# Hybrid attention encoder: low parts of turned probabilities and of meta keys on GpSimd, inverse sums half a tile sooner

## The chip, the core and the metric

The kernel runs on one core of a Trainium2 chip. Times are device microseconds (us) of one execution. The core has a matmul engine (TensorE, PE in the profile), a vector engine (VectorE, DVE), a scalar engine (ScalarE, ACT), a general engine (GpSimd, POOL) and SyncE (SP), which issues the DMA transfers here. Each engine works through its own queue in order; an instruction that waits holds back all that stand behind it.

## The reference

Two layers of a transformer-like block on 512 tokens of a grid 64 wide, with 16 meta tokens ahead of them, D = 1024, all in float32:

```python
def hybrid_layer(x, norm_g, w_in, q_norm_g, k_norm_g, rpb, w_o_attn, w_o_na, w_out, cos, sin):
    h = rms_norm(x, norm_g)
    proj = jnp.einsum('bld,de->ble', h, w_in)
    qa, ka, va, za, qb, kb, vb, zb, ga, gb = split_cols(proj)
    qa = apply_axial_rope(rms_norm(qa.reshape(b, l, ATTN_HEADS, HEAD_DIM), q_norm_g), cos, sin)
    ka = apply_axial_rope(rms_norm(ka.reshape(b, l, ATTN_KV_HEADS, HEAD_DIM), k_norm_g), cos, sin)
    ...
    oa = gqa_attention(qa, ka, va) * jax.nn.silu(za)
    ...
    ob = neighbourhood_attention(qb, kb, vb, rpb) * jax.nn.silu(zb)
    ya = jnp.einsum('ble,ed->bld', oa, w_o_attn)
    yb = jnp.einsum('ble,ed->bld', ob, w_o_na)
    mixed = jax.nn.sigmoid(ga) * ya + jax.nn.sigmoid(gb) * yb
    return x + jnp.einsum('bld,de->ble', mixed, w_out)
```

`gqa_attention` is the global branch: 8 query heads, 2 key heads, softmax over all 528 keys. `neighbourhood_attention` is the window branch: 8 heads, each query sees a window of 8 x 16 grid neighbours and the meta keys.

## The kernel before

**Precision.** Every matmul operand is split into a high part, a float32r cast, and a low part, the difference. A product is three matmuls: high by high, high by low, low by high (lines 325 to 327 in `product`).

**The main stream.** Each layer streams 58 chunks of weights through TensorE. A chunk comes in two halves of 128x512: the raw weights by DMA (line 235), the high part `whi` by a cast on ScalarE (line 240), the low part `wlo` by a subtraction on GpSimd (line 241). `weights` keeps three halves ahead of the product that needs them. The product of a chunk covers the tokens in two spans of 264 where the meta tokens are still needed (layer 0, and the keys and values of layer 1) and else in one span of 512; a span of the first kind, and half of one of the second, is half a tile of work and ends with a `tick`.

**The side work.** The attention branches run beside this stream. Two objects of the class `Side` hold the units of the global branch (`side_gqa`) and the heads of the window branch (`side_na`). At each tick they write down the steps that are due; a unit starts every four ticks, and its steps stand at numbers of ticks after its start, in the tables `GQA_AT` and `NA_AT`. A scheduler then orders each engine's queue from the written order, priorities and what waits for what.

**A unit of the global branch** (`global_unit`) is one query head and a pair of 128-query blocks; there are 16 in each layer, and two smaller ones of the meta queries in layer 0. Its steps:

- *scores*: two matmul groups into `S` (lines 556, 557), scaling and maximum on VectorE (837), exponential on ScalarE (841) into `P`, with the sums of the exponentials in `suma`.
- *turn*: P is transposed in blocks of 32 on VectorE (867) and written to DRAM (870). *back*: four reads bring it back turned (877), one more the rows of the meta keys (880, tile `pm`).
- *split*: each of two `split_part` casts half of the turned P to `pth` on ScalarE (193) and subtracts to `ptl` on VectorE (194), both in the helper `split`. *ends*: `split_ends` does the same for the meta keys' rows, two casts of 32x128 on ScalarE (896) and two subtractions on VectorE (898), into a kept tile `ga`.
- *sums*: nine matmuls (905) of values by `pth`, `ptl` and `ga` into `av`. ScalarE and VectorE then collect it into the branch's output (`combine`, lines 769 and 773).

**Inverse sums.** The probabilities aren't divided; instead the gate `za` of a pair of heads is multiplied by the inverse sums. The last unit of a pair carries the three steps of `divided_later`: *turned* takes the reciprocal (808), transposes it (809) and writes it with four DMAs (811); *spread* reads it back to all partitions with two (817); *multiplied* multiplies `za` on GpSimd (822). `gated` (777) then multiplies the output by za. The table's entry "divide" places these three. The window branch has its own entry and its own copy of the steps, with `zb`.

**A head of the window branch** (`windowed_head`) writes scores over a bias tile, transposes the probabilities on TensorE in three steps (tiles `ta`, `tb`, `tc`, line 129), splits them (`tah`/`tal`, `tbh`/`tbl`, line 194), and in layer 0 also moves a small tile of meta probabilities, `tm` to `mm` (lines 1019, 1020). The transposed tiles share a few PSUM banks, so that a transposition waits until an earlier tile has been read. Its values are split into `VB`.

GpSimd has the 210 `wlo`, and beside them the multiplications of line 822, the split of the windows' keys (533, tile `KB`) and of their queries (514), and the last products' kept weights (272).

Of the kernel before, what the change touches and what calls it, by code (L numbers as in the profile page):

```python
# [11 lines left out]
F32 = mybir.dt.float32  # L12
# [21 lines left out]
DEPTH = 2  # L34


GQA_AT = ({"scores": (0, 1), "turn": (1, 2), "back": 3, "split": (5, 5), "ends": 5, "divide": (3, 4, 6), "sums": (7, 7)},
          {"scores": (0, 1), "turn": (1, 2), "back": 3, "split": (5, 5), "ends": 5, "divide": (3, 4, 6), "sums": (7, 7)})
NA_AT = ({"stages": (0, 2, 5, 5, 5, 7), "values": (3, 4), "divide": (3, 4, 6)},
         {"stages": (0, 2, 4, 5, 5, 7), "values": (3, 4), "divide": (3, 4, 6)})  # L40

# [54 lines left out]
def trunk_kernel(ctx: ExitStack, tc: tile.TileContext, xT, w, gn, gf, bias, rope, out):  # L96
    nc = tc.nc
# [15 lines left out]
    def slot(tag, name, dt=F32):  # L113
        n = NKEY if tag in ("KB", "KR", "K", "E") else NTOK
        t = slots.tile([P, n], dt, tag=tag, bufs=BUFS[tag], name=name)
        return t[:, :NTOK] if tag == "E" else t
# [54 lines left out]
    def pad_tile(kind):  # L171
        padded[kind].rotate(1)
        return padded[kind][0]
# [14 lines left out]

    split_at = {}

    def split(hi, lo, src):
        with tc.high_priority():
            split_at["hi"] = nc.scalar.copy(hi, src)  # L193
            split_at["any"] = nc.vector.tensor_sub(lo, src, hi.bitcast(F32))  # L194

    def newton(out, x, tmp):
        nc.vector.scalar_tensor_tensor(tmp, out, -0.5, out, op0=ALU.mult, op1=ALU.mult)
# [236 lines left out]
    first, ends = {}, ((0, HALF), (HALF, NTOK))  # L434
# [19 lines left out]
    for l in range(DEPTH):  # L454
# [22 lines left out]
        def rotated(c, g, full, name):  # L477

            n, j = NTOK if full else NREAL, c - QA

            if name == "k":
                keys.append(slot("KR", f"{name}{l}_{c}")[:, :NTOK + NMETA])
            q = slot("E", f"{name}{l}_{c}") if name == "q" else keys[0][:, NMETA:]
            sq = slot("G", f"{name}s{l}_{c}")
            qh, ql = slot("G", f"{name}h{l}_{c}", F32R), slot("G", f"{name}l{l}_{c}", F32R)
            for ps, a, b in project(c, full):
                with ExitStack() as held:
                    if "last" in evac:
                        held.enter_context(tc.issue_after(evac["last"].ins))
                    nc.scalar.mul(q[:, a:b], ps, g)  # L490
                    nc.scalar.activation(qh[:, a:b], ps, AF.Square)
                    evac["last"] = nc.scalar.activation(sq[:, a:b], ps, AF.Square)
            with tc.high_priority():
                evac["low"] = nc.vector.tensor_sub(ql[:, :n], sq[:, :n], qh[:, :n].bitcast(F32))
            side_gqa.later(NORM_AT[l]["squares"][j], lambda: sum_squares(j, n, qh, ql))

            def rotate():
                sh = slot("G", f"{name}r{l}_{c}")
                nc.vector.stream_shuffle(sh[:, :n], q[:, :n], [(i + 16) % 32 for i in range(32)])
                nc.vector.tensor_mul(sh[:, :n], sh[:, :n], sin[:, :n])  # L500
                nc.vector.tensor_mul(q[:, :n], q[:, :n], cos[:, :n])
                nc.vector.tensor_add(q[:, :n], q[:, :n], sh[:, :n])

            return q, rotate
# [86 lines left out]
        qs, turn = [], None  # L591
        for j in range(4):
# [3 lines left out]
            with tc.issue_after(evac["low"].ins):  # L596
                if l == 0 and j == 0:
                    turn = rotate
                else:
                    if turn:  # L600
                        turn()
                    turn = None
# [14 lines left out]
        k, rotate = rotated(KA, g_k[l], True, "k")  # L617
# [125 lines left out]
        v = scaled(VA, f"va{l}")  # L743
# [103 lines left out]
        def global_unit(kv, parts, n, name, done):  # L847

            width = n * len(parts)
            per = min(4, 512 // width)  # L850

            first_token = (0, NMETA)
            c = {"t": []}

            def scores(i):
                q, qs, scale, total = parts[i]
                if i == 0:
                    c["both"] = slots.tile([P, 2 * NTOK], F32, tag="M", bufs=BUFS["M"], name=f"P{name}")
                    c["p"] = [c["both"][:, NTOK * t:NTOK * (t + 1)] for t in range(len(parts))]
                softmax(c["p"][i], q, qs, kv, NMETA - first_token[i], n, scale, total, f"{name}_{i}")  # L860

            def turn(i):

                a, b = (0, NREAL) if i == 0 and len(parts) > 1 else (NREAL * i, NREAL * i + NREAL + 32)
                if len(parts) == 1:
                    nc.gpsimd.memset(c["both"][:n, NTOK:b], 0.0)
                nc.vector.transpose(c["both"][:n, a:b], c["both"][:n, a:b])  # L867
                if i == len(parts) - 1:
                    c["there"] = dpool.tile([P, 2 * (NREAL + 32)], F32, tag="turned", bufs=3, name=f"turn{name}")
                    nc.sync.dma_start(c["there"][:n, :b], c["both"][:n, :b])  # L870

            def back():

                w, there = width * 4, c["there"][:n].rearrange("(b j) (t f) -> j t b f", j=32, t=2)
                for q in range(4):
                    r = slice(32 * q, 32 * q + 32)
                    nc.sync.dma_start(c["both"][r, :w].rearrange("j (t b x) -> j t b x", t=len(parts), x=P),
                                      there[:, :len(parts), :, P * q:P * q + P])
                c["meta"] = tiny.tile([32, P], F32, tag="meta", name=f"pm{name}")
                nc.sync.dma_start(c["meta"][:, :n].rearrange("j (b i) -> j b i", i=32),  # L880
                                  c["there"][:n].rearrange("(b j) f -> j b f", j=32)[:, :, NREAL:NREAL + 32])

            def split_part(kt):
                v = c["both"][:, :width * 4].rearrange("p (x k i) -> p x k i", k=4, i=32)[:, :, kt:kt + per]
                th, tl = slot("G", f"pth{name}_{kt}", F32R), slot("G", f"ptl{name}_{kt}", F32R)
                split(*(t[:, :width * per].rearrange("p (k x i) -> p x k i", k=per, i=32) for t in (th, tl)), v)
                for i in range(per):
                    for v in (th, tl):
                        c["t"].append((VA2[:, kt + i, kv], v[:, width * i:width * (i + 1)]))

            def split_ends():

                tm, m = pad_tile("ga"), c["meta"][:, :n]
                with tc.high_priority():
                    for t in range(len(parts)):
                        nc.scalar.copy(tm[32 * t:32 * t + 32, n * t:n * (t + 1)], m)
                    for t in range(len(parts)):
                        nc.vector.tensor_sub(tm[64 + 32 * t:96 + 32 * t, n * t:n * (t + 1)], m, tm[:32, :n].bitcast(F32))  # L898
                c["t"].append((VA2[:, 4, kv], tm[:, :width]))

            def sums(first, last):
                if first == 0:
                    c["av"] = bank(ps_a, f"av{name}", "avg")[:, :width]
                for i in range(first, last):
                    nc.tensor.matmul(c["av"], rows2(c["t"][i][0]), c["t"][i][1], start=i == 0, stop=i == 8)  # L905
                if last == 9:
                    done(c["av"])

            steps = [(at, lambda i=i: scores(i)) for i, at in zip(range(len(parts)), GQA_AT[l]["scores"])]
            for i, at in zip(range(len(parts)), GQA_AT[l]["turn"][-len(parts):]):  # L910
                steps.append((at, lambda i=i: turn(i)))
            steps.append((GQA_AT[l]["back"], back))
            n_t = 4 // per
            for i, (at, then) in enumerate(zip(GQA_AT[l]["split"][:n_t], GQA_AT[l]["sums"][-n_t:])):
                steps.append((at, lambda kt=per * i: split_part(kt)))
                f = 2 * per * (i + 1)
                steps.append((then, lambda a=2 * per * i, b=f + (f == 8): sums(a, b)))
            steps.append((GQA_AT[l]["ends"], split_ends))
            return sorted(steps, key=lambda x: x[0])

# [25 lines left out]
        def start_unit(hd, i):  # L946
# [6 lines left out]
            if g == 6:  # L953
                steps += zip(GQA_AT[l]["divide"], divided_later(sums_a[j], lambda: zgate[j], f"a{l}_{j}"))
            return sorted(steps, key=lambda x: x[0])
# [147 lines left out]
        for j in range(4):  # L1103
            kvq[j] = {"k": slot("KR", f"kb{l}_{j}")}
            kb = kvq[j]["k"]
            for ps, a, b in project(KB + j, True):
# [5 lines left out]
                else:  # L1112
                    i, e = NREAL - HD - a, NREAL - a
# [39 lines left out]
        for m in range(8 + LAG):  # L1153
# [9 lines left out]
            if m >= LAG:  # L1163
                ma = slot("G", f"ma{l}_{m - LAG}")
                hi, lo = two("M", f"mx{l}_{m}", F32R)
# [20 lines left out]
        for m in range(8):  # L1186
# [3 lines left out]
            x = xr[m]  # L1190
# [28 lines left out]
    sums = tiny.tile([P, 50], F32, tag="mh", bufs=1, name="sums")  # L1219
    acc, ms, rx = sums[:, :12].rearrange("p (t i) -> p t i", i=3), sums[:, 12:16], sums[:, 16:20]  # L1220
    h2 = D // 4
    for f in range(2):
        for t in range(4):
            x = xs[f, t]
# [30 lines left out]
            else:  # L1255
                r, x, x0 = rx[:, t:t + 1], y[:, :2 * h2], xs[0, t][:, :2 * h2]
# [58 lines left out]
```

## Time and profile before

| | |
|---|---|
| median of 3 runs | 853.73 us |
| lowest and highest | 852.26 and 855.82 us |
| the profiled execution | 855.46 us |
| its span in the trace | 853.1 us |
| granted TensorE clock, mean | 0.992 |

The profile shows one execution. For each engine it gives the busy time, the share of the span and the number of instructions. A group of instructions is a line of code, an engine, an operation and its tiles (output <- inputs), with its shape and count, the busy time in us, the mean of one in ns, and after the bar the idle time of the engine just before them and what ended it. In a timeline the columns are start, duration, engine, line, operation and tiles; square brackets give the idle time before it and what it waited for. In a table by windows each engine has its busy time and, in brackets, its count; then come the granted clock, the DMA's busy share and GB/s.

### The profile page before, as it was taken

Reading aid. Unit: us, or ns where it says so; the run is one execution under the profiler, and the core shown is the slowest. Engines: PE = TensorE matmul, PEld = TensorE weight load, DVE = VectorE, ACT = ScalarE, POOL = GpSimd, SP = SyncE. Lnnn points to the kernel's source line nnn. Section 1 sums busy time; section 2 is a strip of 40 time slices with the busy share of each in tenths; the row PEclk is TensorE's granted clock in tenths of the full one; section 3 lists DMA queues with packets and bytes.
Section 4 is the critical chain, followed back from the end, with each engine's and each line's share of the span. In section 5 each row is a group of like instructions: output and inputs, shape, how many; then the busy total and the mean of one; then the engine's idle time right before and its main releaser. Section 6 shows DMA issues by size and latency. Waiting matters only on the chain.

```text
span 853.1 us, 16107 instructions
## 1 busy us (share of the span) xinstructions
PE 825.1 (97%) x5662; PEld 762.1 (89%) x5662; DVE 552.0 (65%) x1218; ACT 473.7 (56%) x1137; POOL 382.6 (45%) x296
## 2 busy tenths in 40 slices
PE   9999899989999999899999999999999999999997
PEld 9999899989999999899998989898987778878786
DVE  7976658777776675436447657777777657555633
ACT  8654677566764555333435456576757645543422
POOL 1663343343343333545765554443534433445851
PEclk9999999999999999999999999999999999999999
DMA  7277464566544564334555575657476655544502
GB/s 275 90 194 215 122 183 122 172 205 169 169 139 137 164 184 145 112 100 144 147 143 130 142 212 161 170 165 238 124 206 172 193 163 169 169 151 145 176 13 99
DMA packets 113249, 135.00 MB, mean 158 GB/s; under 512 B 31888, under 2 KB 66192, under 8 KB 113168
## 3 DMA queue, kind: packets, MB, share of 16 engines
q1 hardware_dynamic: 112448, 132.90, 53.0%
q8 instruction: 45, 0.74, 0.4%
q10 hardware_dynamic: 720, 1.06, 0.3%
q14 instruction: 36, 0.29, 0.1%
HBM read 98.50 MB, written 21.84 MB: 141 GB/s over the span
## 4 chain that ended last, share of the span: by engine, by line
PE 78%; DVE 8%; ACT 6%; issue 4%; DMA 2%; SPq 1%; POOL 1%; POOLq 0%; ACTq 0%; DVEq 0%
PE pp L327 16%; PE pp L325 16%; PE pp L326 16%; PE av L905 4%; PE y L327 3%; PE y L326 3%; PE y L325 3%; PE avb L1052 2%; DVE ptl L194 2%; PE pf L1234 2%; PE pf L1236 2%; PE pf L1235 2%; PE S L556 2%; PE S L557 1%; DVE ga L898 1%
## 5 line engine op out<-in xcount | busy, mean ns | idle before, releaser
L241 POOL TENSOR_TENSOR wlo<-raw,whi 128x512 fp32r<-128x512 f32 x210 | 289.2, 1386 | 404.7 <-ACT whi L240 325.0
L325 PE MATMUL pp<-hh,whi 128*128 128x264 f32 (+3 forms) x1040 | 326.6, 314 | 2.7 <-DVE mg L1131 1.5
L327 PE MATMUL pp<-hh,wlo 128*128 128x264 f32 (+3 forms) x1040 | 326.2, 314 | 1.3 <-POOL wlo L241 1.2
L326 PE MATMUL pp<-hl,whi 128*128 128x264 f32 (+3 forms) x1040 | 324.3, 312 | 0.0
L327 PEld LDWEIGHTS pp<-hh,wlo 128*128 128x128 f32 x1040 | 196.8, 189 | 12.9 <-POOL wlo L241 2.1
L325 PEld LDWEIGHTS pp<-hh,whi 128*128 128x128 f32 x1040 | 196.5, 189 | 12.4 <-DVE mg L1131 1.7
L326 PEld LDWEIGHTS pp<-hl,whi 128*128 128x128 f32 x1040 | 197.0, 189 | 9.5
L240 ACT CAST whi<-raw 128x512 fp32r<-128x512 f32 x210 | 127.6, 618 | 109.1 <-PE pp L326 41.1
L867 DVE STREAM_TRANSPOSE P<-P 128x512 f32<-128x512 f32 x64 | 46.4, 727 | 36.4 <-ACT P L841 35.7
L194 DVE TENSOR_TENSOR ptl<-P,pth 128x512 fp32r<-128x512 f32 x64 | 53.8, 841 | 5.4 <-ACT pth L193 4.7
L837 DVE CUSTOM_DVE_ANT_1 P<-S,r 128x528 f32<-128x528 f32 x64 | 44.9, 701 | 16.0 <-PE S L557 15.1
L1131 DVE TENSOR_TENSOR mg<-pp,rbc 128x264 f32<-128x264 f32 (+1 forms) x48 | 24.8, 517 | 39.0 <-PE pp L327 38.5
L841 ACT ACTIVATE P<-P,st 128x528 f32<-128x528 f32 x64 | 47.2, 737 | 1.9
L1132 ACT ACTIVATE mg<-mg 128x264 f32<-128x264 f32 (+1 forms) x48 | 23.7, 494 | 35.0 <-DVE mg L1131 34.8
L992 ACT ACTIVATE bias<-bias,stb 128x208 f32<-128x208 f32 (+1 forms) x64 | 31.0, 486 | 20.0 <-DVE stb L990 19.9
L193 ACT CAST pth<-P 128x512 fp32r<-128x512 f32 x64 | 39.3, 614 | 0.1
L840 ACT ACTIVATE st<-st 128x1 f32<-128x1 f32 x64 | 13.0, 203 | 45.4 <-DVE st L837 44.6
L905 PE MATMUL av<-ptl,VA 128*128 128x256 f32 x128 | 34.1, 294 | 3.3 <-DVE ptl L194 3.1
L326 PE MATMUL pp<-mx,whi 128*128 128x264 f32 x128 | 36.6, 286 | 0.0
L327 PE MATMUL pp<-mx,wlo 128*128 128x264 f32 x128 | 36.4, 284 | 0.0
L325 PE MATMUL pp<-mx,whi 128*128 128x264 f32 x128 | 36.3, 284 | 0.0
L905 PE MATMUL av<-pth,VA 128*128 128x256 f32 x128 | 34.8, 295 | 0.0
(534 smaller groups left out, 1731.6 us busy)
## 6 DMA issues: line engine op xcount, KB each, us to landing
raw<-in_w_dram SPq DMA_DIRECT2D x210, 256.0 KB
turn<-P SPq DMA_DIRECT2D x32, 528.0 KB
P<-turn SPq DMA_DIRECT2D x128, 128.0 KB
bias<-in_bias_dram SPq DMA_DIRECT2D x16, 480.0 KB
KB<-KB SPq DMA_DIRECT2D x24, 272.0 KB
rawl<-in_w_dram SPq DMA_DIRECT2D x16, 256.0 KB
x<-in_xT_dram SPq DMA_DIRECT2D x8, 264.0 KB
xr<-in_xT_dram SPq DMA_DIRECT2D x8, 264.0 KB
```

The source lines that it names most:

```text
L193: split_at["hi"] = nc.scalar.copy(hi, src)
L194: split_at["any"] = nc.vector.tensor_sub(lo, src, hi.bitcast(F32))
L240: cast = nc.scalar.copy(hi, raw)
L241: sub = nc.gpsimd.tensor_sub(lo, raw, hi.bitcast(F32))
L325: nc.tensor.matmul(ps, wh, rh[:, a:b], start=i == 0, stop=False)
L326: nc.tensor.matmul(ps, wh, rl[:, a:b], start=False, stop=False)
L327: nc.tensor.matmul(ps, wl, rh[:, a:b], start=False, stop=i == n - 1)
L837: newest["max"] = nc.vector.tensor_tensor_reduce(p[:n].rearrange("p (i k) -> p i k", i=2), S[:n, :, :HALF], scale[:n].unsqueeze(2).to_broa ...
L841: nc.scalar.activation(p[:n], p[:n], AF.Exp, bias=st[:n, 1:2], scale=1.0, accum_out=st[:n, 2:3] if total is None else total)
L867: nc.vector.transpose(c["both"][:n, a:b], c["both"][:n, a:b])
L905: nc.tensor.matmul(c["av"], rows2(c["t"][i][0]), c["t"][i][1], start=i == 0, stop=i == 8)
L992: nc.scalar.activation(pb[b], pb[b], AF.Exp, bias=st[:, b:b + 1], scale=-1.0, accum_out=total[:, b:b + 1])
```

## The change

Three edits. The subtraction for `ptl` goes from VectorE to GpSimd; so do the two small subtractions of the meta keys' rows into `ga`; and in the global branch each of the three steps of the inverse sums is one tick sooner: 2, 3 and 5 after the start of the pair's last unit, not 3, 4 and 6.

```diff
-GQA_AT = ({..., "divide": (3, 4, 6), "sums": (7, 7)},
-          {..., "divide": (3, 4, 6), "sums": (7, 7)})
+GQA_AT = ({..., "divide": (2, 3, 5), "sums": (7, 7)},
+          {..., "divide": (2, 3, 5), "sums": (7, 7)})
...
-    def split(hi, lo, src):
+    def split(hi, lo, src, eng=nc.vector):
         with tc.high_priority():
             split_at["hi"] = nc.scalar.copy(hi, src)
-            split_at["any"] = nc.vector.tensor_sub(lo, src, hi.bitcast(F32))
+            split_at["any"] = eng.tensor_sub(lo, src, hi.bitcast(F32))
...
             def split_part(kt):
...
-                split(*(... for t in (th, tl)), v)
+                split(*(... for t in (th, tl)), v, nc.gpsimd)
...
             def split_ends():
...
-                        nc.vector.tensor_sub(tm[64 + 32 * t:96 + 32 * t, n * t:n * (t + 1)], m, tm[:32, :n].bitcast(F32))
+                        nc.gpsimd.tensor_sub(tm[64 + 32 * t:96 + 32 * t, n * t:n * (t + 1)], m, tm[:32, :n].bitcast(F32))
```

64 ptl of 128x512 and two of 128x256 move, and 64 ga of 32x128 and two of 32x64. TensorE's order stays nearly as it was. A row of the queues below is a line, an operation, output <- inputs and a shape; the numbers in a name are, for a unit, its head and its pair of blocks (`ptl_0_1_2` is head 0, pair 1, second half), for a weight its chunk and half, and last a running number.

The first place is VectorE's queue in layer 0, where head 0's window tiles are transposed (first what the queue was, then what it is):

```order
L1121 SCALAR_TENSOR_TENSOR qb_1_1406<-pp_11_0_1419,rbc_413 128x264
L194 TENSOR_TENSOR ptl_0_1_0_1455<-P_0_1_1161,pth_0_1_0_1454 128x8x2x32
L194 TENSOR_TENSOR VB_0_1385<-vtc_0_1445,VB_0_1385 80x6x64
L194 TENSOR_TENSOR ptl_0_1_2_1459<-P_0_1_1161,pth_0_1_2_1458 128x8x2x32
L898 TENSOR_TENSOR ga_120<-pm_0_1_1354,ga_120 32x128 x2
L1121 SCALAR_TENSOR_TENSOR qb_1_1406<-pp_11_264_1466,rbc_413 128x264
L1019 CAST mm_124<-tm_0_1501 32x16
L1020 TENSOR_TENSOR mm_124<-tm_0_1501,mm_124 32x16
```

```order
L1121 SCALAR_TENSOR_TENSOR qb_1_1406<-pp_11_0_1419,rbc_413 128x264
L194 TENSOR_TENSOR VB_0_1385<-vtc_0_1445,VB_0_1385 80x6x64
L1121 SCALAR_TENSOR_TENSOR qb_1_1406<-pp_11_264_1466,rbc_413 128x264
L1019 CAST mm_124<-tm_0_1501 32x16
L1020 TENSOR_TENSOR mm_124<-tm_0_1501,mm_124 32x16
```

The two ptl and the two ga no longer stand ahead of `mm`.

The second place is GpSimd's queue in layer 1, around the weights of chunk 20 (before, then after):

```order
L241 TENSOR_TENSOR wlo_20_0_7865<-raw_20_0_7740,whi_20_0_7864 128x512
L533 TENSOR_TENSOR KB_20_8064<-kb_2_7733,KB_20_8064 128x544
L241 TENSOR_TENSOR wlo_20_1_7871<-raw_20_1_7862,whi_20_1_7870 128x512
L241 TENSOR_TENSOR wlo_24_0_7977<-raw_24_0_7868,whi_24_0_7976 128x512
L822 TENSOR_TENSOR za_0_7097<-za_0_7097,sumsa_0_7906 128x512
```

```order
L241 TENSOR_TENSOR wlo_20_0_7868<-raw_20_0_7740,whi_20_0_7867 128x512
L533 TENSOR_TENSOR KB_20_8064<-kb_2_7733,KB_20_8064 128x544
L194 TENSOR_TENSOR ptl_1_1_0_7952<-P_1_1_7685,pth_1_1_0_7951 128x8x2x32
L898 TENSOR_TENSOR ga_120<-pm_1_1_7859,ga_120 32x128 x2
L194 TENSOR_TENSOR ptl_1_1_2_7956<-P_1_1_7685,pth_1_1_2_7955 128x8x2x32
L822 TENSOR_TENSOR za_0_7097<-za_0_7097,sumsa_0_7861 128x512
L241 TENSOR_TENSOR wlo_20_1_7874<-raw_20_1_7865,whi_20_1_7873 128x512
L241 TENSOR_TENSOR wlo_24_0_7978<-raw_24_0_7871,whi_24_0_7977 128x512
```

The unit's four subtractions and the multiplication of `za` now stand ahead of the second half of chunk 20. On ScalarE, at the same place, the casts of that unit come sooner, straight after the cast of `VB` (before, then after):

```order
L193 CAST VB_1_7824<-vtc_1_7896 80x6x64
L840 ACTIVATE st_2_0_0_7916<-st_2_0_0_7916 128x1
L841 ACTIVATE P_2_0_7910,suma_1_7909<-P_2_0_7910,st_2_0_0_7916 128x528
L896 CAST ga_120<-pm_1_1_7851 32x128 x2
L741 CAST VB_1_7824<-VB_1_7824 64x256
L240 CAST whi_20_1_7870<-raw_20_1_7862 128x512
L193 CAST tbh_2_7938<-tb_2_7933 128x256
L193 CAST pth_1_1_0_7951<-P_1_1_7685 128x8x2x32
```

```order
L193 CAST VB_1_7832<-vtc_1_7899 80x6x64
L193 CAST pth_1_1_0_7951<-P_1_1_7685 128x8x2x32
L896 CAST ga_120<-pm_1_1_7859 32x128
L193 CAST pth_1_1_2_7955<-P_1_1_7685 128x8x2x32
L840 ACTIVATE st_2_0_0_7916<-st_2_0_0_7916 128x1
L896 CAST ga_120<-pm_1_1_7859 32x128
L841 ACTIVATE P_2_0_7910,suma_1_7909<-P_2_0_7910,st_2_0_0_7916 128x528
L193 CAST tbh_2_7938<-tb_2_7933 128x256
L792 ACTIVATE na_122<-tc_2_7944,inner 32x128 x2
L240 CAST whi_20_1_7873<-raw_20_1_7865 128x512
```

`pth` of the unit has passed the softmax of the next unit and the cast of `whi_20_1`, which now stands behind it.

More of the change, by code (lines that the diff above doesn't have):

```diff
@@ L34 @@
 DEPTH = 2
-GQA_AT = ({"scores": (0, 1), "turn": (1, 2), "back": 3, "split": (5, 5), "ends": 5, "divide": (3, 4, 6), "sums": (7, 7)},
-          {"scores": (0, 1), "turn": (1, 2), "back": 3, "split": (5, 5), "ends": 5, "divide": (3, 4, 6), "sums": (7, 7)})
+GQA_AT = ({"scores": (0, 1), "turn": (1, 2), "back": 3, "split": (5, 5), "ends": 5, "divide": (2, 3, 5), "sums": (7, 7)},
+          {"scores": (0, 1), "turn": (1, 2), "back": 3, "split": (5, 5), "ends": 5, "divide": (2, 3, 5), "sums": (7, 7)})
 NA_AT = ({"stages": (0, 2, 5, 5, 5, 7), "values": (3, 4), "divide": (3, 4, 6)},
@@ L885, in split_part @@
                 th, tl = slot("G", f"pth{name}_{kt}", F32R), slot("G", f"ptl{name}_{kt}", F32R)
-                split(*(t[:, :width * per].rearrange("p (k x i) -> p x k i", k=per, i=32) for t in (th, tl)), v)
+                split(*(t[:, :width * per].rearrange("p (k x i) -> p x k i", k=per, i=32) for t in (th, tl)), v, nc.gpsimd)
                 for i in range(per):
```

## The prediction

> **What bounds the kernel now.** I read the engines' busy times first, then the chain of work that ended last, both from the page.
>
> ```profile
> PE 825.1 (97%) x5662; PEld 762.1 (89%) x5662; DVE 552.0 (65%) x1218; ACT 473.7 (56%) x1137; POOL 382.6 (45%) x296
> ...
> PE 78%; DVE 8%; ACT 6%; issue 4%; DMA 2%; SPq 1%; POOL 1%; POOLq 0%; ACTq 0%; DVEq 0%
> ```
>
> PE sets the end. The change takes no matmul away, so it can win only what PE stands idle or runs at a lower clock, and it can lose wherever PE starts to wait. The span is 853.1 us and the profiled execution took 855.46 us, so 2.4 us lie around the span; that execution is 1.7 us above the median of the three runs, 853.73 us. I add up differences on the trace and apply them to the median. Next I read PE's waits.
>
> ```profile
> engine line waited for: us in total, times, longest us
> PE tb L129 <- DVE mm L1020: 3.3, 2, 3.0
> PE av L905 <- DVE ptl L194: 3.1, 5, 1.0
> PE y L325 <- DVE mg L1131: 2.5, 1, 2.5
> PE tc L129 <- DVE mm L1020: 2.0, 1, 2.0
> ...
> PE tb L129 <- DVE tal L194: 1.5, 2, 1.0
> PE sm L556 <- DVE tbl L194: 1.3, 1, 1.3
> PE pp L327 <- POOL wlo L241: 1.2, 2, 0.7
> ...
> PE av L905 <- DVE ga L898: 1.0, 1, 1.0
> ```
>
> The waits are short and mostly on DVE. Those on mm, tal and tbl belong to the window branch: PE waits because DVE is busy with something else. Those on ptl and ga are waits for the very subtractions that the change moves. POOL is waited for twice, for 1.2 us. A long wait costs a second time, at the clock; I read that from the windows of 1/40 of the span that contain the three longest.
>
> ```profile
> 85.31:106.64 21.33, 18.29 (x142) 18.10 (x141) 14.61 (x43) 12.97 (x40) 7.54 (x5) 0.92 0.45 122
> 191.95:213.27 21.32, 21.32 (x168) 21.07 (x168) 15.01 (x48) 13.10 (x40) 6.42 (x5) 0.93 0.63 169
> 341.24:362.57 21.33, 18.78 (x140) 18.60 (x141) 8.72 (x15) 7.40 (x14) 11.73 (x9) 0.92 0.38 112
> ```
>
> The first number after PE, DVE, ACT and POOL busy is the granted clock: 0.92, 0.93, 0.92. At full clock each window would have held the same matmuls in 8, 7 and 8% less, about 1.7, 1.5 and 1.7 us.
>
> **What moves, and what one costs.** The groups by shape give the durations.
>
> ```profile
> L194 DVE TENSOR_TENSOR ptl<-P,pth 128x512 fp32r<-128x512 f32 x64 | 53.8, 841 | 5.4 <-ACT pth L193 4.7
> L898 DVE TENSOR_TENSOR ga<-pm,ga 32x128 fp32r<-32x128 f32 x64 | 32.0, 499 | 2.3 <-DMA raw<-in_w_dram 0.7
> L241 POOL TENSOR_TENSOR wlo<-raw,whi 128x512 fp32r<-128x512 f32 x210 | 289.2, 1386 | 404.7 <-ACT whi L240 325.0
> L822 POOL TENSOR_TENSOR za<-za,sumsa 128x512 f32<-128x512 f32 x8 | 11.3, 1408 | 10.1 <-DMA sumsa<-therea 8.4 <-DVE mg L1131 1.8
> L573 POOL COPY qmt<-q 128x16 f32<-128x16 f32 x4 | 2.1, 532 | 3.8 <-DVE q L502 3.8
> ```
>
> DVE gives up 53.8 + 32.0, some 86 us beside the four small ones of the meta units. A ptl on POOL has the shape and the types of wlo, so 1.39 us each, 64 x 1.39 = 89 us. A 32x128 subtraction does not occur on POOL: it lies above the 128x16 copy (0.53) and below wlo (1.39). A line through the two gives 0.53 + 0.86 x 112/496 = 0.72; I take 0.7, an estimate, 64 x 0.7 = 45 us. POOL rises from 383 to about 517 us, 61% of the span, DVE falls to about 466. Neither total is near PE's, so only places count.
>
> **Gains: windows that DVE made late.** The timeline of the longest wait, DVE first, then POOL, then PE:
>
> ```profile
> 93.20 0.67 DVE L194 TENSOR_TENSOR ptl<-P,pth 128x512 fp32r<-128x512 f32 x1
> 93.80 0.54 DVE L194 TENSOR_TENSOR VB<-vtc,VB 80x384 fp32r<-80x384 f32 x1
> 94.26 1.78 DVE L194 TENSOR_TENSOR ptl<-P,pth 128x512 fp32r<-128x512 f32 x1
> 96.05 1.55 DVE L898 TENSOR_TENSOR ga<-pm,ga 32x128 fp32r<-32x128 f32 x2
> 97.64 0.43 DVE L1121 SCALAR_TENSOR_TENSOR qb<-pp,rbc 128x264 f32<-128x264 f32 x1
> 97.99 0.15 DVE L1019 CAST mm<-tm 32x16 fp32r<-32x16 f32 x1
> 98.17 0.17 DVE L1020 TENSOR_TENSOR mm<-tm,mm 32x16 fp32r<-32x16 f32 x1
> ...
> 93.49 3.68 POOL L241 TENSOR_TENSOR wlo<-raw,whi 128x512 fp32r<-128x512 f32 x2 [1.67 <-ACT whi L240]
> ...
> 98.49 0.63 PE L129 MATMUL tb<-ident,bias 128*128 128x128 f32 x4 [3.04 <-DVE mm L1020]
> ```
>
> ptl, ga and ga, 0.67 + 1.78 + 1.55 = 4.0 us, stand ahead of the mm for which PE waits 3.04 us; the second ptl takes 1.78 us instead of 0.67 while wlo runs on POOL. With them gone mm has 1.0 us to spare, and PE does not pause: -3.0, and without the pause no lower clock, -1.7. The sums that need these ptl stand 8 us later in PE's order, so the POOL copies are hidden here. The second place is alike:
>
> ```profile
> 188.00 2.42 DVE L898 TENSOR_TENSOR ga<-pm,ga 32x128 fp32r<-32x128 f32 x2
> ...
> 187.73 2.54 POOL L241 TENSOR_TENSOR wlo<-raw,whi 128x512 fp32r<-128x512 f32 x2 [5.26 <-ACT whi L240]
> ...
> 190.96 0.27 PE L129 MATMUL tc<-ident,bias 128*64 128x128 f32 x1 [2.03 <-DVE mm L1020]
> ```
>
> Two ga of 2.42 us together go, more than the wait: -2.0 and -1.5 at the clock. Of the waits on tal and tbl (1.5 + 1.3) I count half, -1.4, since the moved ones are only part of what DVE does there. The 2.5 us on mg in the gate stage I leave at nothing: what is late there hangs on sums and weights that the change rather delays. Sum of gains: **-9.6 us**.
>
> The Trainium skill says in "SBUF — State Buffer", section "Who interferes with whom", that a DVE instruction with two SBUF inputs and a GpSimd instruction that reads SBUF exclude each other for the whole of an instruction; ptl at 1.78 us beside wlo agrees. By that rule the DVE work that stays, VB for one, waits out the new POOL instructions instead. That is a rival below.
>
> **Costs: sums that already wait.** A unit's sums need both ptl and the ga. Where they follow the probabilities at once, the longer path on POOL is PE's. One of the five waits on ptl, in layer 1, on ACT, POOL, DVE and PE:
>
> ```profile
> 695.25 0.61 ACT L193 CAST pth<-P 128x512 fp32r<-128x512 f32 x1
> ...
> 695.43 1.29 POOL L241 TENSOR_TENSOR wlo<-raw,whi 128x512 fp32r<-128x512 f32 x1 [1.46 <-ACT whi L240]
> ...
> 698.34 0.28 DVE L898 TENSOR_TENSOR ga<-pm,ga 32x128 fp32r<-32x128 f32 x1
> ...
> 698.81 0.31 PE L905 MATMUL av<-ga,VA 128*128 128x256 f32 x1
> ```
>
> DVE was done at 698.62. POOL is free at 696.72, then does ptl, ga, ga, ptl in that order: 1.39 + 0.7 + 0.7 + 1.39 = 4.2, done at 700.9, +2.3 us. Without a wlo in the way it starts at 695.87 and ends at 700.1, +1.4. I take +1.6. PE's waits count six such places (five on ptl, one on ga); in two the DVE copy was itself drawn out beside a wlo, as the 1.78 above, and POOL has the same length. Four x 1.6 = **+6.4 us**. Further units have the probabilities early enough by tenths of a us; against that, a wait at one unit hands time to the next. I let the two cancel. At most, all 32 units would pay 2.3: 74 us, far away since most have their sums later in PE's order; at least nothing, if each stall is repaid.
>
> **Costs: weights behind the new work.** POOL works in order. In layer 1 wlo of chunk 20's second half now stands behind ptl, ga, ga, ptl and za (rows of the change above).
>
> ```profile
> 565.25 0.48 ACT L193 CAST VB<-vtc 80x384 fp32r<-80x384 f32 x1
> ...
> 569.46 1.43 POOL L241 TENSOR_TENSOR wlo<-raw,whi 128x512 fp32r<-128x512 f32 x1 [5.14 <-ACT whi L240]
> ...
> 570.95 0.39 PE L327 MATMUL pp<-hh,wlo 128*128 128x264 f32 x1
> ```
>
> PE took it 0.06 us after it was ready, so every delay counts. ACT's new order puts the pth cast behind VB, done at about 566.3 if P has come back by then (the trace shows no landing); 4.2 for the four and 1.4 for za end at 571.9, wlo at 573.3, 2.4 us after 570.9. Some of the four may start sooner; I take **+1.9**. Three more such places (a second layer-1 weight that PE waits for now, and two of layer 0 late in the window heads and in the gate stage) I put at 0.6 each: **+1.8**. If the pth casts come first and POOL is free, they are zero; if P lands late, each is up to the whole group of 5.6 us.
>
> The earlier inverse sums add nothing: the same reciprocal, transposition, four writes and two reads, one tick sooner. Their cover is the multiplication za, which POOL has time for; SP's queue only sees the small writes swap places with a load. Should they come ahead of their sums, a wait of the size of za's own, 1.4 us, would stand at POOL's head four times a layer; I take nothing.
>
> Sum: -9.6 + 6.4 + 1.9 + 1.8 = **+0.5 us**, or 854.2 by the median; I say **854**.
>
> **The rivals.** *DVE's relief wins.* The waits on mm, tal, tbl and mg all go (3.3 + 2.0 + 1.5 + 1.3 + 2.5, and three clock windows of 4.9), the sums pay only half (+3.2) and weights nothing beyond +3.7: -8.6, 845. For it: each of those waits has ptl or ga ahead of it on DVE or beside it; against it: mg stands in a stage where the sums are late. *POOL's order bounds.* At the places where wlo is now taken within 0.1 us the delay is the whole group, ptl, ga, ga, ptl, za (5.6), twice, and each wait over 2 us costs a clock window of 1.7: 2 x (5.6 + 1.7) = 14.6 instead of 3.7, so +11, 865, slower. It decides as soon as wlo comes over 2 us late; the 0.06 us row speaks for it, POOL's idle 404.7 us before wlo against it. *The exclusion.* The remaining two-input DVE work is stretched as ptl was, by about 1.1 us (1.78 - 0.67), at two of the places where I count a gain and at the four sums: 6 x 1.1 = 6.6 on top of the +0.5, 861. Traces bear it out where the rows above overlap, but there is 86 us less such work on DVE. This is the rule named above. *The waits aren't DVE's queue.* If mm waits for its own transposition or a pad tile instead, the -9.6 go: +10, 864. The row shows mm 0.15 us straight after qb, which speaks against it.
>
> **How the numbers follow.** Differences within 0.5% (4.3 us) are about what a measurement of this kernel can tell from no change. Forecast, within that: 0.36. DVE's relief: 0.33. POOL's order: 0.20. The exclusion: 0.06. No relief: 0.05. So faster 0.33, same 0.36, slower 0.31. Both signs hold most of the chance; the forecast's own range is 850 to 858. The whole range goes from a little beyond the relief to POOL's order: 843 to 866.
>
> **What would show it.** Right: in the profile after, mm at both places ends before PE wants it, the clock windows at 85 and 192 us read 1.0, ptl on POOL has a mean near 1.4 us, and PE's waits name POOL ptl, ga and wlo for some 10 us. Wrong: waits of PE on mm that stay (no relief), waits on wlo of over 2 us with a low clock after them (POOL's order), DVE groups such as tal, VB or mx with longer means (the exclusion), or sums that hardly wait for POOL (relief).

## The result and the profile after

The changed kernel takes 875.03 us (median of 4 runs, 873.95 to 876.76), beside 854.12 us for the kernel before on the same chip: ratio 1.0247, 95% interval 1.0217 to 1.0277. It is 20.9 us slower, and the time lies 9 us above the top of the predicted range. The profiled execution took 874.03 us, its span is 872.3 us, 19.2 us longer than before.

The busy times on the page after:

```profile
PE 830.9 (95%) x5662; PEld 764.7 (88%) x5662; DVE 472.3 (54%) x1086; ACT 473.8 (54%) x1137; POOL 491.2 (56%) x428
```

VectorE fell from 552 to 472 us and GpSimd rose from 383 to 491 (466 and 517 were worked out). GpSimd is far from full, and TensorE still has the same 5662 matmuls; it stands idle more. Its waits:

```profile
engine line waited for: us in total, times, longest us
PE av L905 <- POOL ptl L194: 20.1, 26, 1.6
PE pp L327 <- POOL wlo L241: 4.9, 4, 1.8
PE y L325 <- ACT ob L193: 2.9, 1, 2.9
PE pp L325 <- ACT whi L240: 2.2, 2, 1.2
PE tb L129 <- DVE tal L194: 1.8, 2, 1.4
...
PE tb L129 <- DVE mm L1020: 0.4, 1, 0.4
...
PE pp L325 <- DVE mg L1131: 0.3, 1, 0.3
```

Read against the rows of before: the waits on mm fell from 5.3 to 0.4 us, and the 2.5 us on mg in the gate stage are gone. The waits of a unit's sums rose from 4.1 us (ptl 3.1, ga 1.0) to 20.1, in 26 waits of at most 1.6. The weights' waits rose from 1.2 to 4.9. And the clock: the same two windows as before, then two of 10 us where new waits stand close together (granted clock after the five busy times).

```profile
85.31:106.64 21.33, 21.33 (x179) 21.05 (x177) 12.13 (x43) 15.13 (x43) 13.04 (x13) 1.00 0.57 158
191.95:213.27 21.32, 21.32 (x180) 21.10 (x180) 13.21 (x40) 14.75 (x45) 11.04 (x10) 1.00 0.65 171
320.00:330.00 10.00, 8.07 (x52) 7.82 (x52) 2.35 (x6) 3.97 (x10) 6.45 (x7) 0.83 0.24 83
...
648.00:658.00 10.00, 6.88 (x18) 4.92 (x19) 3.77 (x12) 4.21 (x11) 7.24 (x6) 0.66 0.26 87
```

At 85 and 192 us the clock is whole again (0.92 and 0.93 before), but it is lost elsewhere: 0.83 and 0.66 here. Over the span the mean clock went from 0.992 to 0.987. The time lost by it, as an estimate: 0.013 x 872.3 = 11.3 us, beside 0.008 x 853.1 = 6.8, so 4.5 us more.

One unit of layer 0, on GpSimd and then on TensorE, shows what most of the 26 waits are:

```profile
319.24 1.28 POOL L194 TENSOR_TENSOR ptl<-P,pth 128x512 fp32r<-128x512 f32 x1 [4.53 <-ACT pth L193]
320.59 0.97 POOL L898 TENSOR_TENSOR ga<-pm,ga 32x128 fp32r<-32x128 f32 x2
321.63 1.26 POOL L194 TENSOR_TENSOR ptl<-P,pth 128x512 fp32r<-128x512 f32 x1
...
320.57 0.39 PE L905 MATMUL av<-ptl,VA 128*128 128x256 f32 x1 [0.54 <-POOL ptl L194]
...
322.95 0.38 PE L905 MATMUL av<-ptl,VA 128*128 128x256 f32 x1 [1.40 <-POOL ptl L194]
...
323.41 0.41 PE L905 MATMUL av<-ga,VA 128*128 128x256 f32 x1
```

GpSimd was free for 4.53 us before. No weight stands in the way. The chain ptl, ga, ga, ptl itself takes 3.65 us, from 319.24 to 322.89 (321.63 + 1.26), and TensorE's order has the sums right behind the probabilities: it waits 0.54 us for the first ptl and 1.40 for the second.

### The profile page after: what moved, and what is told of

It is laid out like the page before. It is cut to its first block, busy times and chain, and to the rows that moved or that the text cites. A ratio compares the mean times of both kernels' runs of the same rounds, so it can differ in the third digit from the quotient of the medians.

```text
span 872.3 us, 16228 instructions
## 1 busy us (share of the span) xinstructions
PE 830.9 (95%) x5662; PEld 764.7 (88%) x5662; DVE 472.3 (54%) x1086; ACT 473.8 (54%) x1137; POOL 491.2 (56%) x428
## 3 DMA queue, kind: packets, MB, share of 16 engines
q10 hardware_dynamic: 720, 1.06, 0.3%
## 5 line engine op out<-in xcount | busy, mean ns | idle before, releaser
L241 POOL TENSOR_TENSOR wlo<-raw,whi 128x512 fp32r<-128x512 f32 x210 | 284.7, 1366 | 236.8 <-ACT whi L240 209.9
L194 POOL TENSOR_TENSOR ptl<-P,pth 128x512 fp32r<-128x512 f32 x64 | 83.4, 1306 | 79.3 <-ACT pth L193 64.7
L905 PE MATMUL av<-ptl,VA 128*128 128x256 f32 x128 | 35.6, 305 | 20.2 <-POOL ptl L194 20.1
L905 PEld LDWEIGHTS av<-ptl,VA 128*128 128x128 f32 x128 | 24.1, 188 | 26.7 <-POOL ptl L194 26.4
L773 DVE TENSOR_TENSOR oa<-av,cmb 64x256 f32<-64x256 f32 x32 | 13.5, 421 | 49.0 <-ACT cmb L769 48.7
L326 PE MATMUL pp<-mx,whi 128*128 128x264 f32 x128 | 36.6, 286 | 0.0
L898 POOL TENSOR_TENSOR ga<-pm,ga 32x128 fp32r<-32x128 f32 x64 | 29.8, 466 | 11.7 <-ACT ga L896 7.4
```

The lines of the kernel that those rows point to most:

```text
L194: split_at["any"] = eng.tensor_sub(lo, src, hi.bitcast(F32))
L241: sub = nc.gpsimd.tensor_sub(lo, raw, hi.bitcast(F32))
L326: nc.tensor.matmul(ps, wh, rl[:, a:b], start=False, stop=False)
L898: nc.gpsimd.tensor_sub(tm[64 + 32 * t:96 + 32 * t, n * t:n * (t + 1)], m, tm[:32, :n].bitcast(F32))
```

## The experiments

Theory A: the loss is this chain, TensorE waiting for a unit's low parts on GpSimd, and the half clock after such waits. Theory B: GpSimd's load as such, weights and gates that stand behind the new work. Each run is compared with the kernel before on the same chip.

### The parts alone

```diff
 e1: "divide": (2, 3, 5) alone
 e2: split(..., v, nc.gpsimd) in split_part alone
 e3: nc.gpsimd.tensor_sub(tm[64 + 32 * t:...], ...) in split_ends alone
```

> The inverse sums one tick sooner, nothing else of the change. Theory A (the sums wait: nearly all of the loss is TensorE waiting for the low parts on GpSimd, and the half clock after such waits) and theory B (GpSimd's order: weights and gates stand behind the new subtractions) both say no loss here: 852 to 856 us, ratio 0.998 to 1.003. If it is over 858, the earlier steps themselves cost something, and both are short of a part.

> Only ptl on GpSimd; the meta keys' subtractions and the inverse sums as before. Theory A: after the change the two ga, 0.97 us, lie between the first and the second ptl, and about 14 waits of the sums are over 1 us; each loses about 0.9, so 12 to 14 us of the 21 go: 860 to 864 us, waits on ptl 7 to 9 us. Theory B: ga is a small part of what stands ahead of a weight (0.97 of 3.6 us), so 868 to 873 us.

> Only the meta keys' subtractions on GpSimd. Theory A: they end beside the ptl on VectorE, which loses 32 us of work; no wait longer: 848 to 854 us. Theory B: 45 us fewer on GpSimd than ptl would bring, but still ahead of weights in places: 853 to 858 us.

The inverse sums alone: 856.16 us, ratio 1.0016 (0.9996 to 1.0036), no difference that can be told. The trace shows a trade: the waits on mg fall from 4.0 to 0.3 us, those on wlo rise from 1.2 to 2.6, on tal from 1.9 to 3.1, on the window branch's output `na` from 1.1 to 2.3, and one of 1.4 us on ob is new. ptl alone: 855.27, 1.0011 (0.9992 to 1.0029), none either, where the change as a whole loses 21. ga alone: 842.14, **0.984** (0.9818 to 0.9861): 12.6 us faster than before, and below the ranges of both theories, as ptl alone was.

TensorE's waits with ptl alone, and the ga left on VectorE in that run:

```profile
PE av L905 <- POOL ptl L194: 8.7, 16, 1.7
```

```profile
L898 DVE TENSOR_TENSOR ga<-pm,ga 32x128 fp32r<-32x128 f32 x64 | 56.8, 888 | 5.6 <-ACT ga L896 4.2
```

The waits came out as theory A had them (7 to 9 us), while the time came out 5 us lower than it said: A had not counted that the waits on mm (0.2 us left) and their clock (mean 0.996) are won at the same time. ga takes 888 ns beside ptl on GpSimd, 499 before. What that costs is not shown; the waits on tal are 4.4 us in this run, 1.9 before.

With ga alone on GpSimd, TensorE's waits were:

```profile
PE av L905 <- DVE ptl L194: 2.3, 4, 0.9
...
PE pp L327 <- POOL wlo L241: 1.2, 2, 0.7
...
PE tb L129 <- DVE mm L1020: 0.8, 1, 0.8
```

Here the two engines share a unit: GpSimd does two ga while VectorE does two ptl. The wait on mm is nearly gone as in the change, the sums wait less than before, the weights no more, and the mean clock is 0.995.

### The parts in pairs

```diff
 e10: ptl and ga on GpSimd, "divide": (3, 4, 6)
 e11: ptl on GpSimd, "divide": (2, 3, 5)
 e4:  ga on GpSimd, "divide": (2, 3, 5)
```

> ptl and ga on GpSimd, the inverse sums as before. By the runs so far ptl alone gives +1 us and ga alone -12. Theory A (the sums wait for a GpSimd chain of ptl, ga, ga, ptl, which only exists when both are there): the loss is there without the earlier inverse sums: 868 to 876 us, waits on ptl about 20 us. Theory B (GpSimd's order, weights and gates behind the new work, with za drawn ahead by the earlier steps): about half of it, 855 to 864 us.

> ptl on GpSimd and the earlier inverse sums; the meta keys' subtractions on VectorE. Theory A: as ptl alone, 854 to 859 us. Theory B: the gate's multiplication comes ahead of weights, 860 to 868 us.

> The meta keys' subtractions on GpSimd and the earlier inverse sums; ptl on VectorE. Theory A: as ga alone, 841 to 846 us. Theory B: 848 to 856 us.

| on GpSimd | inverse sums as before | inverse sums sooner |
|---|---|---|
| nothing | 0 | +1.4 us (1.0016) |
| ptl | +0.5 (1.0011) | +9.0 (1.0097; 1.0075 to 1.0119) |
| ga | -12.6 (0.984) | -6.5 (0.9915; 0.9893 to 0.9937) |
| ptl and ga | +9.9 (1.0107; 1.0081 to 1.0133) | +20.9 (1.0247) |

Theory B's ranges contained the two pairs with ptl (863.56 us in 855 to 864, 862.64 in 860 to 868), which theory A had wrong; ga with the sooner inverse sums, 847.2 us, fell between the two. Two things are read from the table. First, ga saves 12.6 us alone and costs 9.4 on top of ptl: the relief is one and the same (ptl alone already takes the waits on mm away), and the second ptl then stands behind ga. With both, waits on ptl are 16.7 us, with ptl alone 8.7:

```profile
PE av L905 <- POOL ptl L194: 16.7, 22, 1.7
```

Second, the inverse sums sooner cost 6 to 11 us as soon as anything of the change is on GpSimd. Between the last pair, with the sooner sums against without, the waits on ptl rise from 16.7 to 20.1 us, those on wlo from 1.8 to 4.9, those on the cast whi from 1.1 to 2.2, and the mean clock falls from 0.991 to 0.987, about 3.6 us: together some 11 us.

### The sums later, and ga behind

```diff
 e5, on top of the change: "sums": (7, 7) -> (8, 8)
 e13, on top of the change:
                     for t in range(len(parts)):
+                        with tc.issue_after(split_at["any"].ins):
                         nc.gpsimd.tensor_sub(tm[64 + 32 * t:...], ...)
```

> The whole change, with every unit's sums one tick (about 6 us of TensorE) later. Theory A: the waits on ptl go, and the half clocks after them: 845 to 855 us, unless the later sums hold up the gate stage at the end of a layer. Theory B: GpSimd's order is the same, 866 to 873 us.

> The whole change, with the two ga of a unit behind its second ptl on GpSimd, not between the two. If it is the place of ga between the ptl that costs (the second ptl 0.97 us later), the loss falls to that of ptl with the earlier inverse sums, 862 to 865 us. If it is the length of GpSimd's chain to the unit's last matmul (theory A as the runs leave it), only the 0.5 us of the four matmuls ahead of ga is won, in some 10 units, the wait moves from ptl to ga: 867 to 873 us.

Sums one tick later: 859.59 us, ratio 1.0062 (1.004 to 1.0084); 15 of the 21 us are back, short of A's 845 to 855, as 9.8 us of waits on ptl stay in 10 places and those on wlo are 6.4. With ga behind: 867.62 us (864.82 to 870.94), 1.0159 (1.0122 to 1.0197). The median lies at the lower edge of what was expected of the chain's length, but the interval reaches down to what was expected of the place of ga (862 to 865), so the two aren't cleanly told apart. The run is 13.4 us above before, so the place of ga is worth some 7.5 us of the 20.9; the rest stays. All other engines' orders are the change's. The waits moved:

```profile
PE av L906 <- POOL ptl L194: 7.5, 16, 1.1
PE pp L327 <- POOL wlo L241: 5.0, 4, 2.0
PE av L906 <- POOL ga L899: 4.6, 11, 0.4
```

### The loss taken apart

Three kernels have the orders of the change on TensorE, VectorE and ScalarE but for a few rows; the fourth (e15) has those of the pair ptl and ga. They differ in what GpSimd computes and what TensorE reads of it. Where ga's subtraction writes into the unread tile, it stands behind the second ptl.

```diff
 e8, neither computed: th = tl = slot("G", f"pth{name}_{kt}", F32R), no subtraction
 e9, ptl computed, not read:
                 for i in range(per):
-                    for v in (th, tl):
+                    for v in (th, th):
 e14, both computed, neither read: as e9, and ga's subtraction writes into that tl
 e15: as e14, "divide": (3, 4, 6)
```

> The low parts of the turned probabilities and of the meta keys are left out; TensorE multiplies the high part twice; the inverse sums as in the change. This is VectorE's relief with no work put on GpSimd. Theory A: mm's waits, the sums' waits and their half clocks all go, weights and gates stay: 834 to 842 us. If it is not under 845, the relief was never worth what the working said.

> The change as it is, but TensorE multiplies the high part of the turned probabilities twice; the low parts are computed on GpSimd as in the change and not read (their product is left out). The order on all engines is that of the change but for a few rows. Theory A: the waits on ptl (20.1 us) go and with them most of the six half-clock windows (about 1.7 us each): 875 - 20 - 7 = 848, 845 to 852 us. Theory B: GpSimd's load is unchanged, so most of the loss stays: 866 to 873 us.

> As the change, with neither low part read: TensorE multiplies the high part of the turned probabilities twice, and the low part of the meta keys is written into an unread tile (both products are left out). TensorE's, VectorE's and ScalarE's orders are those of the change but for a few rows; GpSimd has all its new work. Theory A: the 7.5 us of waits on ga that were left with ptl unread (860.8 us) go too, with about two half clocks: 848 to 852 us. Theory B: they were only the place where GpSimd's load shows, and weights and gates wait instead: 856 to 861 us.

> As the run before it in this pair, with the inverse sums at their old ticks. If the earlier steps cost by bringing za ahead of weights on a loaded GpSimd (waits on wlo 1.8, 1.5 and 1.0 us at three places of the change), 4 us and a half clock or two go: 4 to 7 us below its partner. If they cost only together with the sums' waits, under 2 us.

| | median, us | against before | step |
|---|---|---|---|
| neither low part computed | 837.02 | -17.2 (0.9796; 0.9771 to 0.9821) | -17.2 |
| both computed on GpSimd, neither read | 854.9 | +0.4 (1.0003; 0.999 to 1.0016) | +17.6 |
| ga read too | 860.75 | +6.0 (1.0071; 1.0044 to 1.0097) | +5.6 |
| the change: ptl read too | 875.03 | +20.9 (1.0247) | +14.9 |

Both theories are half right. Without the low parts 17 us are won, inside theory A's 834 to 842. That is VectorE's relief together with sums that wait for no low part: the 4.1 us of waits on ptl and ga of before are in it. GpSimd's load eats all of it, 17.6 us, with nothing of it read; theory A expected the third rung at 845 to 852 and the second at 848 to 852, B the second at 856 to 861 and the third at 866 to 873, and both runs fell between. Reading what GpSimd made costs 5.6 + 14.9 = 20.5 us more, which is about the whole loss against before. The steps hold in this order; the runs don't show that the load alone costs as much when TensorE also waits for the sums.

TensorE's waits with no low part, then with both unread:

```profile
PE pp L327 <- POOL wlo L241: 3.0, 4, 1.0
...
PE y L325 <- ACT ob L193: 1.4, 1, 1.4
```

```profile
PE pp L327 <- POOL wlo L241: 9.8, 7, 2.6
PE y L325 <- ACT ob L193: 2.7, 1, 2.7
```

The mean clock fell from 0.997 to 0.988 between the two: 0.012 x 853.8 - 0.003 x 835.2 = 7.7 us, beside 6.8 + 1.3 of these waits. The longest wait on a weight, on GpSimd and TensorE in the run with both unread:

```profile
634.44 2.51 POOL L194 TENSOR_TENSOR ptl<-P,pth 128x512 fp32r<-128x512 f32 x2 [6.03 <-DMA raw<-in_w_dram]
637.03 0.96 POOL L900 TENSOR_TENSOR ptl<-pm,ga 32x128 fp32r<-32x128 f32 x2
638.07 1.26 POOL L822 TENSOR_TENSOR za<-za,sumsa 128x512 f32<-128x512 f32 x1
639.29 2.96 POOL L241 TENSOR_TENSOR wlo<-raw,whi 128x512 fp32r<-128x512 f32 x2
...
640.61 0.79 PE L327 MATMUL pp<-hh,wlo 128*128 128x512 f32 x1 [2.56 <-POOL wlo L241]
```

GpSimd was idle for 6.03 us and then had 4.8 us of a unit and its gate ahead of the weight for which TensorE waited. In the change itself the weights' waits are smaller (4.9 us); probably because the sums' waits delay TensorE, which gives GpSimd time.

The run with both unread and the inverse sums at their old ticks took 852.24 us (0.9971; 0.9957 to 0.9985), 2.7 us below its partner. It fell between the two expectations. The 2.5 us wait on mg of the kernel before is 5.5 here, where the gate za stands on GpSimd behind the unit's subtractions and some weights:

```profile
PE y L325 <- DVE mg L1133: 5.5, 1, 5.5
PE pp L327 <- POOL wlo L241: 4.5, 6, 1.5
```

So the sooner inverse sums give the wait on mg away and take waits on weights for it (9.8 against 4.5). In the whole change they also lengthen the waits on ptl (16.7 to 20.1 us), which don't exist here; why the cost is 11 us there and only 2.7 here isn't settled beyond that.

### Better divisions of the work

```diff
 e6:  split(..., v, nc.gpsimd if kt == 0 and per == 2 else nc.vector), nothing else of the change
 e12: ga on GpSimd; split(..., v, nc.gpsimd if name in ("0_0_1", "0_1_0", "0_2_1", "0_3_0",
      "0_3_1", "0_4_0", "1_0_0", "1_1_1") else nc.vector); "divide" as before
```

> Only the first ptl of a unit on GpSimd; the second ptl, ga and the inverse sums as before the change. Theory A: the two halves run beside each other, 1.3 us at most in the chain, waits on ptl 3 to 5 us and the window's mm comes sooner: 843 to 851 us. Theory B: half of the weights' delay: 853 to 857 us.

> The meta keys' subtractions on GpSimd, and ptl there only for eight of the 32 units, whose sums stand several us after their probabilities in the profile before; the inverse sums as before. Theory A: no new waits, VectorE freed where the window's tiles wait: as ga alone or up to 3 us less, 838 to 843 us. Theory B: 844 to 850 us.

A unit's first ptl alone on GpSimd: 852.4 us, 0.998 (0.9964 to 0.9996), less gain than theory A said; 3.3 of the 5.3 us of waits on mm stay in that run, in which a ptl and both ga still stand on VectorE. ga on GpSimd, with ptl for eight units whose sums come late: 839.88 us, **0.9834** (0.9809 to 0.9859), inside theory A's 838 to 843. That beats both kernels, but is not told apart from ga alone (0.9818 to 0.9861).

## Why the prediction was wrong

Its terms, with what the trace of the change measured:

| step of the prediction | said, us | measured, us |
|---|---|---|
| waits on mm | -5.0 | 5.3 to 0.4: -4.9 |
| waits on tal and tbl | -1.4 | 2.8 to 1.8: -1.0 |
| half clock | -3.2 | mean 0.992 to 0.987: +4.5 |
| sums that wait | +6.4 | 4.1 to 20.1: +16.0 |
| weights behind the new work | +3.7 | 1.2 to 4.9: +3.7 |
| earlier inverse sums | 0 | +11.0 beside the other two (20.9 - 9.9) |

The first five rows add up to +18.3 us, beside the 19.2 by which the span grew. The last row is a difference of runs and is contained in the rows above it.

**What bounds the kernel** was right: only places count, not GpSimd's share of 56%.

**The gains at the two window places** were right. The first of them, after the change, on VectorE and then TensorE:

```profile
92.96 0.55 DVE L194 TENSOR_TENSOR VB<-vtc,VB 80x384 fp32r<-80x384 f32 x1 [0.75 <-ACT VB L193]
94.51 0.43 DVE L1121 SCALAR_TENSOR_TENSOR qb<-pp,rbc 128x264 f32<-128x264 f32 x1 [1.00 <-PE pp L327]
95.06 0.16 DVE L1019 CAST mm<-tm 32x16 fp32r<-32x16 f32 x1
95.25 0.17 DVE L1020 TENSOR_TENSOR mm<-tm,mm 32x16 fp32r<-32x16 f32 x1
...
95.56 0.63 PE L129 MATMUL tb<-ident,bias 128*128 128x128 f32 x4
```

mm starts 2.9 us sooner, VectorE now idles ahead of it, and TensorE does not wait. mm is done only 0.14 us before TensorE's matmul, though, not the 1.0 us that were said. In the reading of the clock one row was not what it was called: the window from 191.95 us starts after the wait that ended at 190.96 and shows the lower clock behind it.

**The first step that failed is the count in "Costs: sums that already wait".** The prediction charged four of the six places that waited in the trace of before, at 1.6 us each, and let all others "cancel" against time handed from one unit to the next. After the change 26 waits stand at 19 units, 20.1 / 19 = 1.06 us each: the price was, if anything, high, and the count was wrong. A unit for which no wait is listed can be as near the edge as one that has one. The unit shown above was such a one; before the change, on VectorE and TensorE:

```profile
321.43 0.69 DVE L194 TENSOR_TENSOR ptl<-P,pth 128x512 fp32r<-128x512 f32 x1
...
322.18 0.38 PE L905 MATMUL av<-ptl,VA 128*128 128x256 f32 x1
```

Its second ptl was ready at 322.12, 0.06 us before the matmul that reads it. Taken unit by unit from the same trace, 20 of the 32 units had one of their low parts ready less than 1 us before its matmul, and 17 of the 19 that wait after the change are among them. For those 19 the time from the first cast to pth to the end of the second ptl rose from 3.35 to 4.41 us in the mean, and to the end of the last of the four subtractions only from 4.13 to 4.41. So the chain as a whole is hardly longer than it was on VectorE, where it was stretched and mixed with other work; what comes about 1 us late is the second ptl, which on GpSimd has both ga ahead of it. With ga behind it the second ptl is done after 3.38 us again and the last ga after 4.42, and TensorE's waits on the two are 12.1 us, not 20.1. The runs with ptl and ga unread show the size: 20.5 us of time hang on reading the two.

**The second is the clock.** The prediction gave 3.2 us back at the two places and charged nothing for the waits it added; in the change the clock lost 4.5 us more than before. In windows of 10 us over the whole span, beside the kernel's end, the clock is down at three places before, by 1.7 us of time each, and at five after, one of them twice as long.

**The third is "The earlier inverse sums add nothing".** Alone that holds (0.9996 to 1.0036), by a trade of waits. Beside the moved work it costs 6 to 11 us. One place is seen in the trace, the weight of chunk 20 that the prediction worked out by hand:

```profile
570.24 1.29 POOL L194 TENSOR_TENSOR ptl<-P,pth 128x512 fp32r<-128x512 f32 x1 [3.35 <-ACT pth L193]
571.60 0.97 POOL L898 TENSOR_TENSOR ga<-pm,ga 32x128 fp32r<-32x128 f32 x2
572.65 1.29 POOL L194 TENSOR_TENSOR ptl<-P,pth 128x512 fp32r<-128x512 f32 x1
573.90 1.30 POOL L822 TENSOR_TENSOR za<-za,sumsa 128x512 f32<-128x512 f32 x1
575.13 3.78 POOL L241 TENSOR_TENSOR wlo<-raw,whi 128x512 fp32r<-128x512 f32 x3
...
576.48 0.39 PE L327 MATMUL pp<-hh,wlo 128*128 128x264 f32 x1 [1.51 <-POOL wlo L241]
```

The wait is 1.51 us, 1.9 were said; with the inverse sums at their old ticks and the rest of the change there is no wait at this place. **The weights' step** was right in its sum, +3.7, and that is partly luck: the longest of the four waits, 1.83 us at 225.83, stands in layer 0, where 0.6 was put on a place.

**The wait on mg**, left at nothing, went, and a new one of 2.9 us came, in the gate stage of layer 1, behind the window branch's last gate zb on GpSimd:

```profile
683.82 1.31 POOL L194 TENSOR_TENSOR ptl<-P,pth 128x512 fp32r<-128x512 f32 x1
685.08 1.28 POOL L241 TENSOR_TENSOR wlo<-raw,whi 128x512 fp32r<-128x512 f32 x1
686.32 1.26 POOL L822 TENSOR_TENSOR zb<-zb,sumsb 128x512 f32<-128x512 f32 x1
...
689.01 0.80 PE L325 MATMUL y<-ob,whi 128*128 128x512 f32 x1 [2.87 <-ACT ob L193]
```

**The rivals.** "POOL's order" had the right side, but not the mechanism in the change: no wait on a weight was over 1.83 us there. That GpSimd's load can cost much shows only with the low parts unread (17.6 us). "The exclusion" did not show as a price: tal and VB kept their means (0.68 and 0.55 us before and after). "DVE's relief" had about the size that its rival said: gains of 15.5 us before its costs, beside 17.2 with no low part computed, of which 4.1 are the sums' own waits. Moving both operations brought none of it in time; moving ga alone brought 12.6.

The durations: ptl and ga on GpSimd, after the change:

```profile
L194 POOL TENSOR_TENSOR ptl<-P,pth 128x512 fp32r<-128x512 f32 x64 | 83.4, 1306 | 79.3 <-ACT pth L193 64.7 <-DMA bias<-in_bias_dram 6.1 <-DMA raw<-in_w_dram 2.9
L898 POOL TENSOR_TENSOR ga<-pm,ga 32x128 fp32r<-32x128 f32 x64 | 29.8, 466 | 11.7 <-ACT ga L896 7.4
```

1.31 us for 1.39 said, and 0.47 for 0.7; the 0.47 lies below the 128x16 copy of 0.53 that was taken for its lower end. Had they been as long as said, the loss would probably have been larger still; no run shows it.

## What to carry to other kernels

When an operation moves to a slower engine, count every place whose slack is smaller than the delay that the move adds to the operand read there, not only the places that wait in the trace before; here 20 of 32 units had less than 1 us of slack and 19 waited, not 4. Moving one of two operations that feed the same matmuls can let two engines share the work (ga alone: 12.6 us won; ptl alone: no difference), moving both put the second ptl behind ga on one engine (9.9 us lost, 20.9 with the sooner inverse sums). Parts that are harmless alone need a run in pairs when they stand in one queue.

## What the runs showed of the hardware

Short waits close together can cost the clock like one long one: 0.54 and 1.40 us within 2.4 us, at 320 us, were followed by a clock of 0.83 in a window of 10 us, where before the change the waits that it followed were 2 us and longer. They need not: 0.48 and 1.41 us within 2.4 us, at 308 us, were followed by a clock of 1.00 from 310 to 320 us, and so was a single wait of 1.83 us at 226 us. What decides is not shown.

ga of the same shape took 0.47 us on GpSimd in the change, and with ptl left on VectorE

```profile
L898 POOL TENSOR_TENSOR ga<-pm,ga 32x128 fp32r<-32x128 f32 x64 | 40.8, 638 | 85.9 <-ACT ga L896 47.9 <-issue 32.1 <-POOL wlo L241 2.7
```

0.64: the stretching that the prediction read on VectorE's side is there on GpSimd's side too. In that run the 46 ga that overlap a TENSOR_TENSOR on VectorE took 0.71 us in the mean, the other 18 took 0.46; before the change, with ga on VectorE, it was 1.01 for the 19 that overlap one on GpSimd and 0.28 for the other 45. The Trainium skill's rule in "SBUF — State Buffer", "Who interferes with whom", agrees with that and with ga's 888 ns on VectorE beside ptl on GpSimd. In "Perfetto Trace Analysis", "Optimizing Scalar/DVE Operations", the Trainium skill says that offloading between the two engines might not help, for the port they share; here one of two moves helped by 12.6 us, and what undid the pair was the second ptl's place behind ga and GpSimd's queue.
